# First attention laid out class by class: keys and queries stored by token mod 4, neighbour units reading keys in runs of 32, queries kept twice

## The chip, the cores and the metric

The kernel runs as one program on one core of a Trainium2 chip. The metric is the device time of one execution in microseconds (us), the median of several runs. Before the change it is 2000.86 us (3 runs, 2000.85 to 2000.86).

## What is computed

The reference is an encoder of two layers for 1024 tokens of width 1024. Each layer has a token-mixing part and a mixture of 16 experts; a final norm ends it. The change touches one part only: the dilated window attention of layer 0, with 12 heads of width 64. Cut to what matters:

```python
A_PATTERNS = ((128, 1), (512, 4), (2048, 16))

def dilated_band_attention(q, k, v, window, dilation):
    # query t attends t + j*dilation, |j| <= window/(2*dilation)
    ...
def dilated_mixture(q, k, v):
    results = [dilated_band_attention(q, k, v, w, d) for (w, d) in A_PATTERNS]
    outs = jnp.stack([o for (o, _) in results], axis=0)
    lses = jnp.stack([l for (_, l) in results], axis=0)
    wts = jax.nn.softmax(lses, axis=0)
    return jnp.einsum('pbsh,pbshc->bshc', wts.astype(q.dtype), outs)
```

Every head thus looks at its keys three times: 64 neighbours to each side; 64 to each side in steps of 4; 64 to each side in steps of 16. The weights of the mixture make it one softmax over all three sets of keys.

## The kernel before

**Units.** `a_attention` works through 12 heads, and each head through 8 units (96 in all, `u = 8*head + s`). A unit has two blocks of 128 queries by 256 keys. In units s = 0 to 3 (below: class units) r = s is a class of tokens, those with token mod 4 = r; a block takes 128 queries of the class against all its 256 keys, and one mask (`cls`) does the steps of 4 and of 16 together. In units s = 4 to 7 (neighbour units) a block takes 128 neighbouring queries against the 256 keys from 64 before to 64 behind them, under the masks `nat0` to `nat2`. The results of the class units go to `o2c`, those of the neighbour units to `o1`. `bounce` sends `o2c` through DRAM into the order of the tokens (`o2`), and four merge steps weigh the two.

**Precision.** Queries and keys are split into a high and a low part (`k.split`, L148 and L149), and the two halves of the 128 partitions hold hi and lo. `tr` transposes them on TensorE into a PSUM tile `apt` and copies that to `kT` and `qT`. `a_swap` writes a second copy of `kT` with hi and lo swapped, by two DMAs; a block's scores are two matmuls into one half of `ass` (L1190), one against each copy.

**Layout.** In `kT` the 1024 keys lie in the order of the tokens, with 64 zeros at either end; so do the queries in `qT`. A class unit reads both in steps of 4 elements (16 bytes, L1173 and L1174), a neighbour unit without a step (L1169).

**Order of the work.** The order is written by hand (`manual_schedule`): in step t the program emits the exponentials of unit t+1 (ScalarE, L1199), the four transposes of unit t (TensorE, `apP`, L1206) and the copy out of PSUM (ScalarE, `pT`, L1208), the scores of unit t+2 (TensorE) with the masking on VectorE (`sm`, L1192), the copies of the transposes asked for in the step before (`late`), the products with the values of unit t-1 (TensorE, `apO`, L1220) and, after each second one, a copy on VectorE (L1226). Then come the pieces of `prep` for a later head, by the table `plan`: splitting k and q, two transposes each for k and q (L1136, one `apt` of 4 matmuls), the swap. Each engine takes its instructions in this order.

**Loads.** SyncE's queue (SP) issues all loads of a head pair. `load` fetches `qs` and `ks` (one DMA each), `load_v` the values twice: `vc` by classes (four DMAs) and `vn` in runs of 128 tokens shifted by 64 (three DMAs, behind two small memsets on GpSimd). The swaps and the bounce are issued by the same queue, in program order: the swap of the next head stands behind the loads of the next pair. The first head is prepared earlier by `a_first`, while the projections of layer 0 still run.

Of the kernel before, what the change touches and what calls it, by code (L numbers as in the profile page):

```python
# [19 lines left out]
S = 1024  # L20
# [10 lines left out]
def _layout():  # L31
    parts = {}
    cols = []
    n = 0

    def add(name, a):
        nonlocal n
        a = np.asarray(a, np.float32).reshape(128, -1)
        parts[name] = (n, n + a.shape[1])
        cols.append(a)  # L40
        n += a.shape[1]

    p = np.arange(128)
    add("ident", np.eye(128))
    add("slots", np.broadcast_to(np.arange(1, 129), (128, 128)))
    add("pref", p[:, None] <= p[None, :])
    e16 = np.zeros((128, 16))
    e16[p[:32], p[:32] % 16] = 1.0
    add("e16", e16)
    add("prow", p)  # L50
    add("sgn", np.stack([np.where(p < 64, 1.0, -1.0), np.where(p < 32, 1.0, -1.0), np.where(p < 16, 1.0, -1.0)], 1))
    for m in (64, 32, 16):
        sel = np.zeros((128, m))
        sel[m:2 * m] = -np.eye(m)
        add(f"sel{m}", sel)
    w = np.arange(256)
    band = (w[None, :] >= p[:, None]) & (w[None, :] <= p[:, None] + 128)
    for name, ok in (("nat0", band & (w >= 64)), ("nat1", band), ("nat2", band & (w < 192))):
        add(name, np.where(ok, 0.0, NEG))
    cls = np.zeros((128, 2, 256))  # L60
    for hf in range(2):
        l = 128 * hf + p[:, None]
        cnt = (np.abs(l - w[None, :]) <= 64).astype(int) + ((l - w[None, :]) % 4 == 0)
        cls[:, hf] = np.where(cnt == 2, np.float32(np.log(2.0)), np.where(cnt == 1, 0.0, NEG))
    add("cls", cls)

    def table(pos, r, theta):
        half = r // 2
        inv = np.power(np.float32(theta), -np.arange(half, dtype=np.float32) * np.float32(2.0 / r))
        ang = pos.astype(np.float32)[:, None] * inv[None, :].astype(np.float32)  # L70
        return np.cos(ang).astype(np.float32), np.sin(ang).astype(np.float32)

    def chunked(t):
        return t.reshape(8, 128, -1).transpose(1, 0, 2)

    t = np.arange(S)
    for name, tabs in (("ra", [table(t, 16, 500000.0)]), ("rc", [table(t, 32, 500000.0)]),
                       ("rd", [table(t // 64, 32, 10000.0), table(t % 64, 32, 10000.0)])):
# [919 lines left out]
    return T  # L998


def a_keys(nc, qk, hp, qs, ks):
    src, c, w = (qk[0], hp * 128, 512) if hp < 4 else (qk[1], (hp - 4) * 128, 256)
    nc.sync.dma_start(qs, src[:, c:c + 128].rearrange("(c p) d -> p c d", p=128))
    nc.sync.dma_start(ks, src[:, w + c:w + c + 128].rearrange("(c p) d -> p c d", p=128))


def a_values(nc, vd, hp, vn, vc):
    nc.gpsimd.memset(vn[0:64, 0], 0.0)
    nc.gpsimd.memset(vn[64:128, 8], 0.0)
    vv = vd[:, 2 * hp:2 * hp + 2].rearrange("t h d -> t (h d)")  # L1010
    vr = vv.rearrange("(f p r) d -> p r f d", f=2, r=4)
    for r in range(4):
        nc.sync.dma_start(vc[:, 2 * r:2 * r + 2], vr[:, r])
    nc.sync.dma_start(vn[64:128, 0], vv[0:64])
    nc.sync.dma_start(vn[:, 1:8], vv[64:960].rearrange("(c p) d -> p c d", p=128))
    nc.sync.dma_start(vn[0:64, 8], vv[960:1024])
    return {n: t.rearrange("p c (h d) -> p c h d", h=2) for n, t in (("vn", vn), ("vc", vc))}


def a_swap(nc, kT):  # L1020
    for a in (0, 64):
        nc.sync.dma_start(*(kT[p:p + 64, f, 64:64 + S].bitcast(F32) for p, f in ((64 - a, 1), (a, 0))))


def a_first(k, qk, vd, pool, ps, cv):


    nc = k.nc

    def take(name, *shape, dtype=F32):  # L1030
        return pool.tile([128, *shape], dtype, name=name)
    kT, qT = take("kT", 2, 128 + S, dtype=F32R), take("qT", S, dtype=F32R)
# [4 lines left out]
    pair, head = dict(qs=qs, ks=ks, cls=cls), dict(kT=kT, qT=qT)  # L1037
# [8 lines left out]
    def trans(n, dst):  # L1046
        for half in range(2):
            pt = ps.tile([128, 4, 128], F32, name="pt").bitcast(F32R)
            for c in range(4):
                nc.tensor.transpose(pt[:, c], sp[n][:, 4 * half + c].rearrange("p a d -> p (a d)"), k.identr)  # L1050
            pv, sl = pt.rearrange("p a d -> p (a d)"), slice(half * 512, (half + 1) * 512)
            if half:
                nc.vector.tensor_copy(dst[:, sl], pv)
            else:
                nc.scalar.activation(dst[:, sl], pv, AF.Copy)

    def keys():
        trans(0, kT[:, 0, 64:64 + S])
        nc.vector.memset(kT[:, :, 0:64].bitcast(F32), 0.0)
        nc.vector.memset(kT[:, :, 64 + S:].bitcast(F32), 0.0)  # L1060
        split(1, qs)

    def queries():
        a_swap(nc, kT)
        trans(1, qT)
# [14 lines left out]
def a_attention(k, qk, vd, gd, o2d, start, late_work, ready):  # L1080
# [4 lines left out]
    with ExitStack() as ctx:  # L1085
# [26 lines left out]
        def prep(h):  # L1112
# [6 lines left out]
            def split_k():  # L1119
                sp = pq.tile([128, NCH, 2, 64], F32R, name="ksp", bufs=1)  # L1120
                k.split(sp[:, :, 0], sp[:, :, 1], pair[hp]["ks"][:, :, hs])
                d["ksp"] = sp
                d["kT"] = pk.tile([128, 2, 64 + S + 64], F32R, name="kT")
                nc.vector.memset(d["kT"][:, :, 0:64].bitcast(F32), 0.0)
                nc.vector.memset(d["kT"][:, :, 64 + S:].bitcast(F32), 0.0)
# [7 lines left out]
            def tr(dst, src, eng):  # L1133
# [3 lines left out]
                pv = pt.rearrange("p a d -> p (a d)")  # L1137
                if eng:
                    late.append(lambda: nc.vector.tensor_copy(dst, pv))
                else:  # L1140
                    late.append(lambda: nc.scalar.activation(dst, pv, AF.Copy))

            def tk(half):
                tr(d["kT"][:, 0, 64 + half * 512:64 + (half + 1) * 512], lambda c: d["ksp"][:, 4 * half + c], half)

            def tq(half):
                tr(d["qT"][:, half * 512:(half + 1) * 512], lambda c: d["qsp"][:, 4 * half + c], True)
# [10 lines left out]
        def blocks(u):  # L1158
# [1 line left out]
            h, s = divmod(u, 8)  # L1160
            hp, hh = divmod(h, 2)
            d, pr = head[h], pair[hp]
            qT, kT = d["qT"], d["kT"]
            out = []
            for j in range(2):
                if s >= 4:
                    c = 2 * (s - 4) + j
                    out.append((qT[:, c * 128:(c + 1) * 128], [kT[:, f, c * 128:c * 128 + 256] for f in range(2)],
                                k.c("nat0" if c == 0 else "nat2" if c == 7 else "nat1"),  # L1169
                                [pr["vn"][:, c + a, hh, 0:65] for a in range(2)], pr["o1"][:, c, hh]))  # L1170
                else:
                    r = s
                    out.append((qT.rearrange("p (l r) -> p r l", r=4)[:, r, j * 128:(j + 1) * 128],  # L1173
                                [kT[:, f, 64:64 + S].rearrange("p (l r) -> p r l", r=4)[:, r] for f in range(2)],  # L1174
                                pr["cls"][:, j], [pr["vc"][:, 2 * r + a, hh, 0:65] for a in range(2)],
                                pr["o2c"][:, 2 * r + j, hh]))
            return out
# [1 line left out]
        def emit_S(u):  # L1179
# [6 lines left out]
            ss = psS.tile([128, 2, 256], F32, name="ass")  # L1186
            sm = p3.tile([128, 2, 256], F32, name="sm")
            for j, (q, ks, mask, v, dst) in enumerate(bl):
                for f in range(2):
                    nc.tensor.matmul(ss[:, j], q, ks[f], start=(f == 0), stop=(f == 1))  # L1190
# [898 lines left out]
```

## Time and profile before

| | |
|---|---|
| median of 3 runs | 2000.86 us |
| the profiled execution's own time | 1999.71 us |
| its span, first to last instruction | 1997.9 us |
| TensorE matmul busy | 1864.8 us, 93% of the span |
| VectorE busy | 1473.5 us, 74% |
| ScalarE busy | 1244.9 us, 62% |
| mean granted TensorE clock | 0.968 |
| scores of the first attention (L1190), first and last start | 270.8 and 480.9 us |

The profile is of one execution. PE is TensorE's matmuls, PEld its weight loads, DVE is VectorE, ACT is ScalarE, POOL is GpSimd, SP is SyncE, whose rows are DMA issues. Times in rows count from the first instruction. The part that the change touches takes a little over a tenth of the span, from about 271 to 484 us; what precedes it (projections) and follows it (output projection, experts, layer 1) is the same program in both kernels.

### The profile page before, as it was taken

The page shows a single profiled execution, that of the slowest core. Times are in us where ns is not written, and L with a number is a line of the kernel's source. Part 1 is how long each engine was busy: PE and PEld are TensorE (multiplying, and loading weights), DVE is VectorE, ACT ScalarE, POOL GpSimd, SP SyncE. Part 2 cuts the span into 40 slices and gives each one's busy share as a digit, 9 for nine tenths or more (in the row PEclk, how much of TensorE's full clock was granted, in tenths as well). Part 3 has the DMA queues.
Part 4 walks back from the last instruction along what each step waited for, and adds up shares of the span by engine and source line. Part 5 has one row for each costly group of instructions (what it writes and reads, how often), then busy time and mean ns, then how long its engine had stood idle before and what let it go on. Part 6 is the DMA issues. An engine that isn't in the chain of part 4 may idle for free. (4 is left out here: it accounts for less than half of the span.)

```text
span 1997.9 us, 29943 instructions
## 1 busy us (share of the span) xinstructions
PE 1864.8 (93%) x10346; PEld 1568.7 (79%) x10346; DVE 1473.5 (74%) x3160; ACT 1244.9 (62%) x2022; POOL 352.4 (18%) x337
## 2 busy tenths in 40 slices
PE   8999999998995999998999799999997995999995
PEld 6888899997883788886888688888886873888884
DVE  6431246777557999997776688889996558999997
ACT  5322257776232888886634688889885334888884
POOL 0010010002002321211002233322212003212111
PEclk9999999999996999999899899999998997999997
DMA  7232354543473999995426554332213875999986
GB/s 236 69 106 75 116 153 130 140 108 109 158 261 126 377 389 384 385 395 156 134 70 202 114 75 90 60 50 42 53 22 93 288 256 201 391 387 385 387 332 229
DMA packets 214599, 386.32 MB, mean 193 GB/s; under 512 B 71984, under 2 KB 122928, under 8 KB 214448
## 3 DMA queue, kind: packets, MB, share of 16 engines
q1 hardware_dynamic: 190224, 303.95, 46.0%
q0 software_dynamic: 21488, 74.18, 12.2%
q10 hardware_dynamic: 2736, 6.29, 0.9%
q8 instruction: 81, 1.33, 0.3%
q14 instruction: 70, 0.57, 0.2%
HBM read 310.17 MB, written 66.85 MB: 189 GB/s over the span
## 5 line engine op out<-in xcount | busy, mean ns | idle before, releaser
L232 DVE TENSOR_TENSOR lo<-raw,hi 128x1024 fp32r<-128x1024 f32 x260 | 310.1, 1227 | 24.2 <-ACT hi L225 23.0
L225 ACT ACTIVATE hi<-raw 128x1024 fp32r<-128x1024 f32 x269 | 275.2, 1055 | 14.5 <-PE py L643 10.2
L259 PE MATMUL pp<-hi,hT 128*128 128x512 f32 (+2 forms) x576 | 213.4, 371 | 2.3 <-ACT hi L235 2.3
L260 PE MATMUL pp<-lo,hT 128*128 128x512 f32 (+2 forms) x576 | 211.8, 368 | 0.1
L261 PE MATMUL pp<-hi,hT 128*128 128x512 f32 (+2 forms) x576 | 211.4, 367 | 0.0
L1879 DVE TENSOR_REDUCE nm<-css 128x1 f32<-128x1024 f32 x128 | 156.0, 1218 | 41.5 <-PE css L1873 40.8
L149 DVE TENSOR_TENSOR PT<-cpt,PT 128x512 fp32r<-128x512 f32 x256 | 163.1, 678 | 6.1 <-ACT PT L148 3.8
L148 ACT ACTIVATE PT<-cpt 128x512 fp32r<-128x512 f32 x256 | 139.5, 597 | 42.1 <-PE cpt L1897 40.3
L1873 PE MATMUL css<-kT,qT 128*128 128x512 f32 x512 | 151.7, 398 | 10.7 <-ACT pe L1885 9.5
L1885 ACT ACTIVATE pe<-css,nm 128x1024 f32<-128x1024 f32 x128 | 143.6, 1122 | 11.0 <-DVE rinv L1905 7.1
L1897 PE MATMUL cpt<-csident,pe 128*128 128x128 f32 x1024 | 135.5, 275 | 1.0 <-DVE PT L149 0.9
L1897 PEld LDWEIGHTS cpt<-csident,pe 128*128 128x128 f32 x1024 | 117.1, 141 | 16.3 <-DVE PT L149 3.7
L1915 PE MATMUL po<-PT,vv 128*128 128x512 f32 x256 | 113.4, 443 | 13.2 <-DVE o L1923 13.2
L259 PEld LDWEIGHTS pp<-hi,hT 128*128 128x128 f32 x576 | 109.7, 190 | 19.8 <-ACT hi L235 2.7
L260 PEld LDWEIGHTS pp<-lo,hT 128*128 128x128 f32 x576 | 109.6, 190 | 17.8 <-DVE lo L236 0.8
L261 PEld LDWEIGHTS pp<-hi,hT 128*128 128x128 f32 x576 | 109.4, 190 | 17.5 <-DVE hT L149 0.2
L1873 PEld LDWEIGHTS css<-kT,qT 128*128 128x128 f32 x512 | 96.0, 189 | 34.6 <-ACT pe L1885 10.8
L1192 DVE CUSTOM_DVE_ANT_0 sm<-ass,csnat 128x256 f32<-128x256 f32 x176 | 67.3, 420 | 52.0 <-PE ass L1190 45.9
L578 POOL DMA_INDIRECT xs<-hd,idx x32 | 70.2, 2195 | 197.5 <-DVE gt L576 197.5
L1916 PE MATMUL po<-PT,vv 128*128 128x512 f32 x256 | 102.3, 400 | 0.0
L1190 PE MATMUL ass<-kT,qT 128*128 128x256 f32 x384 | 96.4, 381 | 1.0 <-DMA kT<-kT 1.0
L259 PE MATMUL pp<-hi,aTh 128*128 128x512 f32 x208 | 87.3, 420 | 0.4 <-DVE o L1226 0.4
(435 smaller groups left out, 4656.0 us busy)
## 6 DMA issues: line engine op xcount, KB each, us to landing
raw<-in_moe_w_up_dram SPq DMA_DIRECT2D x112, 512.0 KB
raw<-in_moe_w_down_dram SPq DMA_DIRECT2D x110, 512.0 KB
raw<-in_moe_w_gate_dram SPq DMA_DIRECT2D x106, 512.0 KB
attn<-in_moe_w_gate_dram SPq DMA_DIRECT2D x22, 512.0 KB
attn<-in_moe_w_down_dram SPq DMA_DIRECT2D x18, 512.0 KB
raw<-in_even_w_in_dram SPq DMA_DIRECT2D x16, 512.0 KB
hd<-h POOLq DMA_DIRECT2D x16, 512.0 KB, 6.0
attn<-in_moe_w_up_dram SPq DMA_DIRECT2D x16, 512.0 KB
```

Of the source, the lines that this page charges most:

```text
L148: self.nc.scalar.activation(hi, src, AF.Copy)
L149: (eng or self.nc.vector).tensor_tensor(lo, src, hi.bitcast(F32), op=ALU.subtract)
L225: nc.scalar.activation(hv, tv, AF.Copy)
L232: (nc.gpsimd if pool else nc.vector).tensor_tensor(lv, tv, hv.bitcast(F32), op=ALU.subtract)
L259: nc.tensor.matmul(out, ah, bh, start=first, stop=False)
L260: nc.tensor.matmul(out, ah, bl, start=False, stop=False)
L261: nc.tensor.matmul(out, al, bh, start=False, stop=last)
L1873: nc.tensor.matmul(ss[:, n], a[:, sl], m[:, n * 512:(n + 1) * 512], start=(j == 0), stop=(j == len(passes) - 1))
L1879: nc.vector.tensor_reduce(nm, B[b]["ss"], axis=AX.X, op=ALU.max, negate=True)
L1885: nc.scalar.activation(pe, B[b]["ss"], AF.Exp, bias=B[b]["nm"], accum_out=l)
L1897: nc.tensor.transpose(pt[:, kk], B[b]["pe"][:, kc * 128:(kc + 1) * 128], k.ident)
L1915: nc.tensor.matmul(po[g], vv[:, kc], PT[g][:, 0, kc], start=(kc == 0), stop=False)
```

## The change

- `a_keys` loads keys and queries class by class: a chunk of 128 rows now holds 128 tokens of one class. Each of the two loads becomes four DMAs, and the keys come first.
- `kT` becomes 4 classes of 256 keys with 16 zeros at either end of each. A class unit now reads queries and keys without a step.
- A neighbour unit reads its 256 keys as 2 x 4 runs of 32 elements (128 bytes): for each half of 128 tokens, 32 keys from each class. The masks' columns and the rows of `vn` are put in the same order; `vn` is loaded by 12 DMAs instead of 3, and its two memsets cover all 128 partitions.
- The neighbour units' queries have to be in the order of the tokens: a second tile `qN`, written from the same PSUM tile by another copy in steps of 4 elements: two ScalarE instructions for each of heads 1 to 11, two on VectorE for the first head.
- The swap moves four runs of 1 KB for each partition instead of one of 4 KB.

```diff
+    wk = 128 * (w // 128) + 4 * (w % 32) + w % 128 // 32
     for name, ok in (("nat0", band & (w >= 64)), ("nat1", band), ("nat2", band & (w < 192))):
-        add(name, np.where(ok, 0.0, NEG))
+        add(name, np.where(ok, 0.0, NEG)[:, wk])
...
+PAD = 16
 def a_keys(nc, qk, hp, qs, ks):
     src, c, w = (qk[0], hp * 128, 512) if hp < 4 else (qk[1], (hp - 4) * 128, 256)
-    nc.sync.dma_start(qs, src[:, c:c + 128].rearrange("(c p) d -> p c d", p=128))
-    nc.sync.dma_start(ks, src[:, w + c:w + c + 128].rearrange("(c p) d -> p c d", p=128))
+    for t, c0 in ((ks, w + c), (qs, c)):
+        v = src[:, c0:c0 + 128].rearrange("(f p r) d -> p r f d", f=2, r=4)
+        for r in range(4):
+            nc.sync.dma_start(t[:, 2 * r:2 * r + 2], v[:, r])
 def a_values(nc, vd, hp, vn, vc):
-    nc.gpsimd.memset(vn[0:64, 0], 0.0)
-    nc.gpsimd.memset(vn[64:128, 8], 0.0)
+    nc.gpsimd.memset(vn[:, 0], 0.0)
+    nc.gpsimd.memset(vn[:, 8], 0.0)
...
-    nc.sync.dma_start(vn[64:128, 0], vv[0:64])
-    nc.sync.dma_start(vn[:, 1:8], vv[64:960].rearrange("(c p) d -> p c d", p=128))
-    nc.sync.dma_start(vn[0:64, 8], vv[960:1024])
+    for r in range(4):
+        p = 32 * r
+        nc.sync.dma_start(vn[p + 16:p + 32, 0], vv[0:64].rearrange("(l r) d -> r l d", r=4)[r])
+        nc.sync.dma_start(vn[p:p + 32, 1:8], vv[64:960].rearrange("(c l r) d -> r l c d", l=32, r=4)[r])
+        nc.sync.dma_start(vn[p:p + 16, 8], vv[960:1024].rearrange("(l r) d -> r l d", r=4)[r])
 def a_swap(nc, kT):
     for a in (0, 64):
-        nc.sync.dma_start(*(kT[p:p + 64, f, 64:64 + S].bitcast(F32) for p, f in ((64 - a, 1), (a, 0))))
+        nc.sync.dma_start(*(kT[p:p + 64, f, :, PAD:PAD + 256].bitcast(F32) for p, f in ((64 - a, 1), (a, 0))))
+def a_pads(nc, kT):
+    nc.vector.memset(kT[:, :, :, 0:PAD].bitcast(F32), 0.0)
+    nc.vector.memset(kT[:, :, :, PAD + 256:].bitcast(F32), 0.0)
+def two(v):
+    return v.rearrange("p (r l) -> p r l", r=2)
...
             def tr(dst, src, eng, nat=None):
...
                 if eng:
                     late.append(lambda: nc.vector.tensor_copy(dst, pv))
                 else:
                     late.append(lambda: nc.scalar.activation(dst, pv, AF.Copy))
+                if nat is not None:
+                    late.append(lambda: nc.scalar.activation(nat, pv, AF.Copy))
...
                 if s >= 4:
-                    out.append((qT[:, c * 128:(c + 1) * 128], [kT[:, f, c * 128:c * 128 + 256] for f in range(2)],
+                    out.append((qN[:, c * 128:(c + 1) * 128],
+                                [kT[:, f, :, 32 * c:32 * c + 64].rearrange("p r (a l) -> p a r l", a=2) for f in range(2)],
...
-                    out.append((qT.rearrange("p (l r) -> p r l", r=4)[:, r, j * 128:(j + 1) * 128],
-                                [kT[:, f, 64:64 + S].rearrange("p (l r) -> p r l", r=4)[:, r] for f in range(2)],
+                    out.append((qT[:, 256 * r + j * 128:256 * r + (j + 1) * 128],
+                                [kT[:, f, r, PAD:PAD + 256] for f in range(2)],
```

On TensorE no instruction is added, dropped or moved. Two engines get more instructions.

ScalarE before, around the third head's split of k and q (`o_2336` is a buffer of `o1`, `pe` the exponentials, `pT` the copy of the transposed ones):

```order
104 L1199 ACTIVATE pe<-sm,o_2336 128x256 x2
105 L1208 ACTIVATE pT<-apP 128x512
106 L1199 ACTIVATE pe<-sm,o_2336 128x256 x2
107 L1208 ACTIVATE pT<-apP 128x512
108 L148 ACTIVATE ksp<-ks 128x8x64
109 L1199 ACTIVATE pe<-sm,o_2336 128x256 x2
110 L1208 ACTIVATE pT<-apP 128x512
111 L148 ACTIVATE qsp<-qs 128x8x64
```

and of the change, the same place:

```order
104 L1227 ACTIVATE pe<-sm,o_2354 128x256 x2
105 L1236 ACTIVATE pT<-apP 128x512
106 L1165 ACTIVATE qN<-apt 128x2x256
107 L1227 ACTIVATE pe<-sm,o_2354 128x256 x2
108 L1236 ACTIVATE pT<-apP 128x512
109 L1165 ACTIVATE qN<-apt 128x2x256
110 L150 ACTIVATE ksp<-ks 128x8x64
111 L1227 ACTIVATE pe<-sm,o_2354 128x256 x2
112 L1236 ACTIVATE pT<-apP 128x512
113 L150 ACTIVATE qsp<-qs 128x8x64
```

Two copies `qN<-apt` stand in front of the exponentials of the units that follow; everything else keeps its place.

SP's queue before, from the swap of one head over the loads of the next pair to the swap of the next head (`kT<-kT` is the swap, `o2d<-o2c` the bounce):

```order
36 L1022 DMA kT<-kT 64x1024 x2
37 L1003 DMA qs<-qka 128x8x128
38 L1004 DMA ks<-qka 128x8x128
39 L1013 DMA vc<-vd 128x2x132 x4
40 L1014 DMA vn<-vd 64x132
41 L1015 DMA vn<-vd 128x7x132
42 L1016 DMA vn<-vd 64x132
43 L1022 DMA kT<-kT 64x1024 x2
```

and of the change, from the same swap, as far as the fourth of twelve `vn` loads:

```order
54 L1033 DMA kT<-kT 64x4x256 x2
55 L1012 DMA ks<-qka 128x2x128 x4
56 L1012 DMA qs<-qka 128x2x128 x4
57 L1022 DMA vc<-vd 128x2x132 x4
58 L1025 DMA vn<-vd 16x132
59 L1026 DMA vn<-vd 32x7x132
60 L1027 DMA vn<-vd 16x132
61 L1025 DMA vn<-vd 16x132
```

Between the two swaps stand 24 load issues instead of 9, for the same bytes, the keys ahead of the queries.

## Rows read from the trace of the kernel before

**Rows 1.** The page, busy time of TensorE over the whole span (share, instructions)

```profile
PE 1864.8 (93%) x10346; PEld 1568.7 (79%) x10346; DVE 1473.5 (74%) x3160; ACT 1244.9 (62%) x2022; POOL 352.4 (18%) x337
```

**Rows 2.** Stretches (us): busy time of each engine (instructions), granted clock, DMA share, GB/s

```profile
410.00:445.00 35.00, 35.00 (x286) 34.95 (x285) 24.46 (x95) 24.90 (x55) 2.27 (x3) 1.00 0.49 123
445.00:480.00 35.00, 34.63 (x271) 33.83 (x270) 27.23 (x95) 26.94 (x56) 1.92 (x1) 1.00 0.22 62
```

**Rows 3.** Timeline of PE, scores only: start, us, line, tile, shape, count

```profile
307.63 1.29 PE L1190 MATMUL ass<-kT,qT 128*128 128x256 f32 x4
...
310.30 1.29 PE L1190 MATMUL ass<-kT,qT 128*128 128x256 f32 x4
...
312.63 1.29 PE L1190 MATMUL ass<-kT,qT 128*128 128x256 f32 x4
...
317.06 0.72 PE L1190 MATMUL ass<-kT,qT 128*128 128x256 f32 x4
...
319.15 0.72 PE L1190 MATMUL ass<-kT,qT 128*128 128x256 f32 x4
...
320.92 0.72 PE L1190 MATMUL ass<-kT,qT 128*128 128x256 f32 x4
...
340.53 1.29 PE L1190 MATMUL ass<-kT,qT 128*128 128x256 f32 x4
```

**Rows 4.** Groups by line, shape (262 to 490): count, busy us, mean ns

```profile
L1190 PE MATMUL ass<-kT,qT 128*128 128x256 f32 x384 | 96.4, 381 | 1.0 <-DMA kT<-kT 1.0
...
L1141 ACT ACTIVATE kT<-apt 128x512 fp32r<-128x512 f32 x11 | 6.4, 585 | 0.0
...
L261 PE MATMUL pp<-hi,hT 128*128 128x256 f32 x26 | 7.3, 281 | 0.0
...
L261 PE MATMUL pp<-hi,aTl 128*128 128x512 f32 x5 | 2.0, 395 | 0.0
```

**Rows 5.** Tile gpm (gMLP), operand in runs of 64: ns least/median/most

```profile
L261 PE MATMUL gpm<-vh,wT x4: 388/391/398, 114.7 to 133.6; 128*128 128x512 f32 x4
```

**Rows 6.** Timeline of SP's DMA issues, loads of the third pair

```profile
313.25 1.11 SPq L1022 DMA_DIRECT2D kT<-kT  x2
314.41 0.61 SPq L1003 DMA_DIRECT2D qs<-qka  x1
...
316.43 4.63 SPq L1013 DMA_DIRECT2D vc<-vd  x4
...
322.26 0.83 SPq L1016 DMA_DIRECT2D vn<-vd  x1
331.11 1.12 SPq L1022 DMA_DIRECT2D kT<-kT  x2
```

**Rows 7.** Timeline of ACT, same loads arriving [idle before, releaser]

```profile
319.14 0.91 ACT L1199 ACTIVATE pe<-sm,o 128x256 f32<-128x256 f32 x2 [0.19 <-DVE o L1192]
319.95 0.57 ACT L1208 ACTIVATE pT<-apP 128x512 f32<-128x512 f32 x1
...
323.31 0.63 ACT L148 ACTIVATE ksp<-ks 128x512 fp32r<-128x512 f32 x1 [1.43 <-DMA ks<-qka]
...
325.13 0.61 ACT L148 ACTIVATE qsp<-qs 128x512 fp32r<-128x512 f32 x1
```

**Rows 8.** Timeline of PE, second head's first scores

```profile
285.89 0.57 PE L1190 MATMUL ass<-kT,qT 128*128 128x256 f32 x1
287.46 1.05 PE L1190 MATMUL ass<-kT,qT 128*128 128x256 f32 x3 [0.99 <-DMA kT<-kT]
```

**Rows 9.** Timeline of SP, that head's swap

```profile
282.24 1.12 SPq L1022 DMA_DIRECT2D kT<-kT  x2
```

**Rows 10.** Line L399, ACT reading in steps of 2 elements

```profile
L399 ACT ACTIVATE h<-xt,rstd x2: 1194/1195/1196, 614.8 to 1646.6; 128x1024 f32<-128x1024 f32 x2
```

**Rows 11.** The page, a dense ACT copy of that size

```profile
L225 ACT ACTIVATE hi<-raw 128x1024 fp32r<-128x1024 f32 x269 | 275.2, 1055 | 14.5 <-PE py L643 10.2
```

**Rows 12.** Timeline of DVE, near the end of the stage

```profile
462.03 1.94 DVE L232 TENSOR_TENSOR lo<-raw,hi 128x1024 fp32r<-128x1024 f32 x1
```

More of the change, by code (lines that the diff above doesn't have):

```diff
@@ L1031, in take @@
         return pool.tile([128, *shape], dtype, name=name)
-    kT, qT = take("kT", 2, 128 + S, dtype=F32R), take("qT", S, dtype=F32R)
+    kT, qT, qN = take("kT", 2, 4, 2 * PAD + 256, dtype=F32R), take("qT", S, dtype=F32R), take("qN", S, dtype=F32R)
     qs, ks = take("qs", NCH, 128), take("ks", NCH, 128)
@@ L1036, in a_first @@
     sp = {}
-    pair, head = dict(qs=qs, ks=ks, cls=cls), dict(kT=kT, qT=qT)
+    pair, head = dict(qs=qs, ks=ks, cls=cls), dict(kT=kT, qT=qT, qN=qN)
     def load():
@@ L1050, in trans @@
                 nc.tensor.transpose(pt[:, c], sp[n][:, 4 * half + c].rearrange("p a d -> p (a d)"), k.identr)
-            pv, sl = pt.rearrange("p a d -> p (a d)"), slice(half * 512, (half + 1) * 512)
+            pv, rs = two(pt.rearrange("p a d -> p (a d)")), slice(2 * half, 2 * half + 2)
             if half:
-                nc.vector.tensor_copy(dst[:, sl], pv)
+                nc.vector.tensor_copy(dst[:, rs], pv)
             else:
-                nc.scalar.activation(dst[:, sl], pv, AF.Copy)
+                nc.scalar.activation(dst[:, rs], pv, AF.Copy)
+            if nat is not None:
+                nc.vector.tensor_copy(nat[:, rs], pv)
     def keys():
-        trans(0, kT[:, 0, 64:64 + S])
-        nc.vector.memset(kT[:, :, 0:64].bitcast(F32), 0.0)
-        nc.vector.memset(kT[:, :, 64 + S:].bitcast(F32), 0.0)
+        trans(0, kT[:, 0, :, PAD:PAD + 256])
+        a_pads(nc, kT)
         split(1, qs)
@@ L1064, in queries @@
         a_swap(nc, kT)
-        trans(1, qT)
+        trans(1, qT.rearrange("p (r l) -> p r l", r=4), qN.rearrange("p (l r) -> p r l", r=4))
     def rest():
@@ L1122, in split_k @@
                 d["ksp"] = sp
-                d["kT"] = pk.tile([128, 2, 64 + S + 64], F32R, name="kT")
-                nc.vector.memset(d["kT"][:, :, 0:64].bitcast(F32), 0.0)
-                nc.vector.memset(d["kT"][:, :, 64 + S:].bitcast(F32), 0.0)
+                d["kT"] = pk.tile([128, 2, 4, 2 * PAD + 256], F32R, name="kT")
+                a_pads(nc, d["kT"])
             def split_q():
@@ L1131, in split_q, with tr @@
                 d["qT"] = pk.tile([128, S], F32R, name="qT")
-            def tr(dst, src, eng):
+                d["qN"] = pk.tile([128, S], F32R, name="qN")
+            def tr(dst, src, eng, nat=None):
                 pt = psT.tile([128, 4, 128], F32R, name="apt")
@@ L1136, in tr @@
                     nc.tensor.transpose(pt[:, c4], src(c4).rearrange("p a d -> p (a d)"), k.identr)
-                pv = pt.rearrange("p a d -> p (a d)")
+                pv = two(pt.rearrange("p a d -> p (a d)"))
                 if eng:
@@ L1141, in tr @@
                     late.append(lambda: nc.scalar.activation(dst, pv, AF.Copy))
+                if nat is not None:
+                    late.append(lambda: nc.scalar.activation(nat, pv, AF.Copy))
             def tk(half):
-                tr(d["kT"][:, 0, 64 + half * 512:64 + (half + 1) * 512], lambda c: d["ksp"][:, 4 * half + c], half)
+                tr(d["kT"][:, 0, 2 * half:2 * half + 2, PAD:PAD + 256], lambda c: d["ksp"][:, 4 * half + c], half)
             def tq(half):
-                tr(d["qT"][:, half * 512:(half + 1) * 512], lambda c: d["qsp"][:, 4 * half + c], True)
+                rs = slice(2 * half, 2 * half + 2)
+                tr(d["qT"].rearrange("p (r l) -> p r l", r=4)[:, rs], lambda c: d["qsp"][:, 4 * half + c], True,
+                   d["qN"].rearrange("p (l r) -> p r l", r=4)[:, rs])
             L[0].append(split_k)
@@ L1162, in blocks @@
             d, pr = head[h], pair[hp]
-            qT, kT = d["qT"], d["kT"]
+            qT, qN, kT = d["qT"], d["qN"], d["kT"]
             out = []
@@ L1188, in emit_S @@
             for j, (q, ks, mask, v, dst) in enumerate(bl):
+                o = ss[:, j] if len(ks[0].shape) == 2 else ss[:, j].rearrange("p (a r l) -> p a r l", a=2, r=4)
                 for f in range(2):
-                    nc.tensor.matmul(ss[:, j], q, ks[f], start=(f == 0), stop=(f == 1))
+                    nc.tensor.matmul(o, q, ks[f], start=(f == 0), stop=(f == 1))
             for j, (q, ks, mask, v, dst) in enumerate(bl):
```

2 lines of the change are left out of this document (1 added, 1 removed).

## Prediction

> **What bounds the kernel now.** I read the page first: matmuls are busy for 93% of the span [rows 1], so a stage is paid for by TensorE unless its own rows say otherwise. The stage of the change lies between 270.8 us (first scores) and about 484 us. The busy times by stretch are the second view [rows 2]: between 410 and 445 us PE is busy for 35.00 of 35 us at a granted clock of 1.00 (the 2.4 GHz level), VectorE for 24.46, ScalarE for 24.90, the DMA engines for about half. The three stretches of 35 us before it read alike; the last one, 445 to 480, is different: VectorE 27.23, PE 34.63.
>
> The third view is PE's timeline, scores alone [rows 3]. From the first matmul of one unit's scores to that of the next, I read 2.67 us (307.63 to 310.30) and 2.33 (310.30 to 312.63) behind class units, 2.09 (317.06 to 319.15) and 1.77 (319.15 to 320.92) behind neighbour units; the longer of each pair has four extra transposes of `prep` in it. These four periods recur almost to the hundredth all along the stage. PE therefore never waits there; it sets the pace. A class unit costs 2.33 - 1.77 = 0.56 or 2.67 - 2.09 = 0.58 us more, although it does the same number of columns: its four score matmuls take 1.29 us against 0.72. What differs is the step of 16 bytes in both operands.
>
> **The change, part by part.**
>
> *Class units without a step.* 12 heads x 4 units = 48. If each comes down to a neighbour unit's period, PE saves 48 x 0.57 = 27.4 us. The bounds: all of it, or nothing, if something else than the step made them slow. I take all: dense matmuls of 256 columns with two-part operands take 281 ns on this PE, the mean of the scores is 381 [rows 4], which is what half slow and half dense gives.
>
> *Neighbour units in runs of 32.* No row shows runs of 32. The gMLP's matmuls read 512 columns in runs of 64 and take 391 ns [rows 5]; dense ones of that size take 395 [rows 4]. So runs of 64 cost nothing. The other end is that runs of 32 cost as much as a step of 4 does, 0.57 us for each of 48 neighbour units. I take nothing, since 32 is far nearer to 64 than to 1.
>
> The SBUF page of the Trainium skill ("SBUF — State Buffer", Door 1: The DMA port swizzle) says that memory lines are 16 bytes wide, that an access in the same line goes at full speed and a crossing to a new line is penalised. It also says that one may step over 4 fp32 values for free; by that the class units would not be slow and the change would be worth 0. Rows 3 show 1.29 us against 0.72 at just this step, so I hold to the first half of the rule. By that half, runs of 32 fill 8 whole lines, but each value of `qN` goes to a line of its own, which is the first rival's case.
>
> *The copies to `qN`.* 22 on ScalarE. A dense copy of that size out of PSUM takes 585 ns [rows 4]. ScalarE rows with a step know only 8 bytes: 1195 ns for 1024 elements [rows 10] against 1055 dense [rows 11], 13% more. Bounds: 0.585 (no price) and 1.17 us (doubled, as the class scores nearly are); I take 0.6. The cover is ScalarE's idle time. A pair of heads is 16 units; 8 x 1.77 + 8 x 2.33 + 8 x 0.33 = 35.4 us now, 30.9 after. ScalarE does about 24.90 x 35.4/35 = 25.2 us per pair, and 27.6 with four copies: 89% of the new period. VectorE comes to 24.7 us, 80%. So the sums fit, but locally it is narrow: five units in a row of each head have an extra ScalarE instruction (two qN, two splits, one key copy). A unit's copy starts 0.81 us after its exponentials and takes 0.57 [rows 7], 1.38 together; with 0.585 for the extra one five units are 9.83 us, and PE needs 2.1 + 1.77 + 1.77 + 2.1 + 2.1 = 9.84. Just hidden, and the three units that follow have nothing extra. If that cover is gone, what ScalarE has over is PE's wait. The two VectorE copies for the first head fall into a time in which VectorE waits for the first scores: nothing.
>
> *Loads on SP.* Now the 9 load issues of a pair run from 314.41 to 323.09, the next swap is issued at 331.11, 17.86 us after the last one [rows 6]. Four class units lie between the swaps, so the next swap will be due 15.6 us after the last. After it about 9.7 us pass before its scores want it (first scores of that head at 340.53 [rows 3], second matmul a little later), since only neighbour units lie there. The swap's own landing is read at the second head: issue at 282.24 [rows 9], the second score matmul runs only at 287.46 behind DMA `kT<-kT` [rows 8], 5.2 us. So the loads may end about 4.5 us after the swap is due: 15.6 + 4.5 - 1.2 = 18.9 us for 24 issues, 0.79 each. An unhindered issue takes 0.61; where the queue is backed up, the four of `vc` take 4.63, 1.16 each [rows 6]. Bounds of the 24: 8.7 us (same bytes) and 27.8. I take 24 x 0.6 = 14.4: no wait. The one new wait among them, `vn` on GpSimd's memset, has `vn` loads, the next swap and the bounce behind it, but the memset runs while SP still issues `vc`.
>
> *Keys first.* Now `ks`, behind `qs`, lands when its split begins, at 323.31 after 1.43 us of idle ScalarE [rows 7]. Afterwards the keys' 512 KB go first and the queries land at about 323.3; their split is called at 325.13 now, at about 325.13 - 1.43 = 323.7 once ScalarE need not wait for the keys. Hidden with little to spare. The 1.43 us themselves buy nothing, since PE did not wait.
>
> *Where class units gain less.* At the start, loads that wait for the buffers stand ahead of the second head's swap, while the four first class units bring its use about 2 us nearer; today PE waits 0.99 us for it [rows 8]. Bounds 0 to 2 us lost; I take 1. At the end, VectorE is nearly full (27.23 us [rows 2]), with splits of weights of 1.94 us [rows 12] between the masks; 8 class units are emitted in that stretch, 4.6 us. I count 2 as lost, bounds 0 to 4.
>
> Sum: 27.4 - 1 - 2 = 24.4, and 0.4 for small waits of the five later pairs: 24.0. The profiled execution takes 1999.71 us (its span 1997.9 and 1.8 around it), so 1975.7; it stands 1.15 us under the median of the runs, so 1976.9 for the median. I say 1977. Nothing behind the stage changes and its loads hang on instructions of the stage, so it moves forward as it is.
>
> **Rivals.**
>
> *ScalarE takes over.* If writing in steps doubles the copies, the five units need 9.83 + 2 x 0.585 = 11.0 us against PE's 9.84: 1.16 late per head, 13 us over 11 heads. Scores are emitted two units ahead and absorb some of it; I take half, 6.5: 1983.5, and 1990 at the worst. For: 16 bytes is the step at which PE slows. Against: PE at that step still takes 256 columns in 1.29/4 = 0.32 us, 0.8 per ns, and the copy asks for 512 elements in 0.585 us, 0.9 per ns.
>
> *The change does not do what it says.* If runs of 32 are as slow as steps, 48 x 0.57 come back: 2001, no change. Against: rows 5.
>
> *SP's queue becomes the bound.* Place: swap of the next head behind 24 issues. At 1.16 us each they end 27.8 us after they begin, 8.9 later than allowed; five pairs make 45 us, less the 24 gained: 2022. It costs from 0.79 us per issue on and outweighs the gain from about 0.99 (18.9 + 24/5 = 23.7 us for 24). For: rows 6 hold issues of that length. Against: those were held up by bytes ahead of them, which are the same bytes in both kernels.
>
> **How the numbers follow.** The forecast gets 0.70, ScalarE 0.14, no change 0.06, SP 0.10. The forecast's own range is 1972.5 (no loss: 2000.86 - 27.4 = 1973.5, and the 0.99 us of rows 8) to 1981 (start and end at their worst). To hold 8 in 10 it has to reach over the middle of ScalarE's case: 1972.5 to 1987. A difference under 0.2% (4 us) cannot be told from none here. Faster 0.85, same 0.05, slower 0.10.
>
> **What would show it.** Class units' scores in 0.72 us and their periods 1.77 and 2.1; neighbour units unchanged at 0.72 (if they rise to 1.29, the second rival). `qN` copies near 0.6 us and no idle PE behind `pe`; if PE waits for exponentials in the units after them, the first rival. The SP row from a pair's first load to the next swap shorter than 17 us, and no score matmul behind `kT<-kT` except at the second head; if there are such waits in each pair, the third. The forecast is wrong if the stage, 210 us from first to last scores, shrinks by less than 18.

## The result and the profile after

The changed kernel takes 1985.81 us (median of 4 runs, 1981.82 to 1987.59) against 2000.86 before: ratio 0.9919, 95% interval 0.9902 to 0.9936. Its profiled execution took 1985.63 us (span 1983.6). On another chip, run again (the fifth experiment), it took 1981.89 against 1991.50: 0.9953, 0.9936 to 0.9969. The time lies inside the range 1972.5 to 1987, 9 us above the 1977 forecast; but in the part that was changed, it will be seen, only a third of the forecast gain arrived (7.8 of 24 us).

The page's busy times, which answer to [rows 1]: ScalarE's have gone up by 13.6 us, TensorE's down by 19.1.

```profile
PE 1845.7 (93%) x10346; PEld 1541.2 (78%) x10346; DVE 1471.7 (74%) x3162; ACT 1258.5 (63%) x2044; POOL 351.7 (18%) x337
```

Busy times by stretch (columns as in [rows 2]):

```profile
410.00:445.00 35.00, 33.84 (x294) 31.65 (x292) 26.60 (x98) 29.27 (x60) 2.20 (x3) 1.00 0.53 139
445.00:480.00 35.00, 31.35 (x246) 29.84 (x246) 21.49 (x79) 26.35 (x52) 3.30 (x2) 0.90 0.13 33
```

TensorE is no longer busy all the time: 33.84 of 35 us where it had 35.00. ScalarE went from 24.90 to 29.27. In the last stretch the granted clock is 0.90: a spell at 0.5 (1.2 GHz) begins at 456 us and lasts 6.8, at a place where the kernel before had none.

The groups by line between 262 and 490 us, which answer to [rows 4]:

```profile
L1218 PE MATMUL ass<-kT,qT 128*128 128x256 f32 x192 | 35.0, 305 | 0.8 <-DMA kT<-kT 0.8
L1218 PE MATMUL ass<-kT,qN 128*128 128x256 f32 x192 | 34.7, 302 | 0.0
L1165 ACT ACTIVATE qN<-apt 128x512 fp32r<-128x512 f32 x22 | 24.1, 1096 | 14.7 <-DVE qT L1161 14.7
```

Class units (`qT`) and neighbour units (`qN`) now cost TensorE the same, 69.7 us together against 96.4. But a copy into `qN` takes 1096 ns, not 600, and in front of these copies ScalarE sat idle for 14.7 us, until VectorE's copy `qT` was done. (The records of neighbouring instructions overlap a little, so the busy time of ScalarE grows by less than the 24.1 us of the copies.)

How the size and the wait reach TensorE is seen in the second pair of heads, while the queries of its second head are prepared, in three timelines (start, us, ..., idle before and its releaser). ScalarE:

```profile
313.99 0.58 ACT L1236 ACTIVATE pT<-apP 128x512 f32<-128x512 f32 x1
315.65 1.10 ACT L1165 ACTIVATE qN<-apt 128x512 fp32r<-128x512 f32 x1 [1.08 <-DVE qT L1161]
316.54 0.87 ACT L1227 ACTIVATE pe<-sm,o 128x256 f32<-128x256 f32 x2
```

VectorE, the copy that it waited for:

```profile
314.94 0.68 DVE L1161 CAST qT<-apt 128x512 fp32r<-128x512 f32 x1
```

TensorE:

```profile
314.77 0.71 PE L1218 MATMUL ass<-kT,qN 128*128 128x256 f32 x4
315.32 1.00 PE L1248 MATMUL apO<-vc,pT 128*128 128x65 f32 x8
317.07 0.83 PE L1234 MATMUL apP<-csident,pe 128*128 128x128 f32 x4 [0.74 <-ACT pe L1227]
317.65 0.73 PE L1218 MATMUL ass<-kT,qN 128*128 128x256 f32 x4
...
319.80 0.72 PE L1218 MATMUL ass<-kT,qT 128*128 128x256 f32 x4
...
322.08 0.71 PE L1218 MATMUL ass<-kT,qT 128*128 128x256 f32 x4
...
324.17 0.72 PE L1218 MATMUL ass<-kT,qT 128*128 128x256 f32 x4
```

ScalarE is free at 314.57, the queries' transposes have ended, but the copy begins at 315.65, right behind VectorE's (314.94 to 315.62). It takes 1.10 us; the exponentials behind it begin at 316.54, and the transposes that need them idle 0.74 us. The period 314.77 to 317.65 is 2.88 us, where [rows 3] have 1.77 for a neighbour unit without `prep`.

The waits of the whole stage (engine, line, waited for: us in total, times, longest):

```profile
PEld apP L1234 <- ACT pe L1227: 15.0, 41, 2.3
ACT qN L1165 <- DVE qT L1161: 14.7, 12, 1.5
...
PE apP L1234 <- ACT pe L1227: 7.6, 10, 2.1
```

The time from the first unit's scores to the last unit's is called the stage below. Its two ends before, and then after the change:

```profile
270.80 2.15 PE L1190 MATMUL ass<-kT,qT 128*128 128x256 f32 x8
...
480.51 0.72 PE L1190 MATMUL ass<-kT,qT 128*128 128x256 f32 x4
```

```profile
271.23 1.11 PE L1218 MATMUL ass<-kT,qT 128*128 128x256 f32 x8
...
473.18 0.72 PE L1218 MATMUL ass<-kT,qN 128*128 128x256 f32 x4
```

The stage went from 209.7 to 201.95 us, 7.8 us less, and the second pair of heads (from unit 16's scores to unit 32's, "the pair" below) from 35.58 to 33.49. The other 7 us of the first comparison lie behind the stage, in unchanged code (see the section on why the prediction was right and wrong).

### The profile page after: what moved, and what is told of

Read it like the earlier page. It is cut to its first block, busy times and chain, and to the rows that moved or that the text cites. A ratio compares the mean times of both kernels' runs of the same rounds, so it can differ in the third digit from the quotient of the medians.

```text
span 1983.6 us, 30146 instructions
## 1 busy us (share of the span) xinstructions
PE 1845.7 (93%) x10346; PEld 1541.2 (78%) x10346; DVE 1471.7 (74%) x3162; ACT 1258.5 (63%) x2044; POOL 351.7 (18%) x337
## 5 line engine op out<-in xcount | busy, mean ns | idle before, releaser
L227 ACT ACTIVATE hi<-raw 128x1024 fp32r<-128x1024 f32 x269 | 275.3, 1055 | 14.3 <-PE py L645 9.5
L150 ACT ACTIVATE xh<-tp 128x512 fp32r<-128x512 f32 x64 | 38.1, 599 | 78.3 <-PE tp L590 52.4
```

Of the source, the lines that this page charges most:

```text
L150: self.nc.scalar.activation(hi, src, AF.Copy)
L227: nc.scalar.activation(hv, tv, AF.Copy)
```

## The experiments

Theory 1: ScalarE's queue, with the size of the copies into `qN` and the wait ahead of each, paces the units and eats most of the gain. Rivals: the gain is lost at the stage's end and in the clock; or to SP's queue. Runs with a ratio are each compared with the kernel before on the same chip; its median was 1994.51 us for e1 to e4, 1991.50 for e5 to e8, 2004.61 for e9 to e12. e8, e10, e11 and e12 ran once each, so their totals have no interval; their stages are compared, which in the two profiles of the changed kernel differ by 0.15 us.

**e1, no copy into `qN`.**

```diff
-                if nat is not None:
-                    late.append(lambda: nc.scalar.activation(nat, pv, AF.Copy))
...
-                    out.append((qN[:, c * 128:(c + 1) * 128],
+                    out.append((qT[:, c * 128:(c + 1) * 128],
```

> The changed kernel without any copy into qN: the neighbour units read qT, so their queries are the wrong ones (this part of the computation is changed). Theory 1 (the 22 ScalarE copies of 1.1 us, each with about 0.67 us of waiting for VectorE's qT copy ahead of it, pace the units): the pair of heads from unit 16 to unit 32 goes from 33.49 us to 30.8 to 31.5, the wait of the probabilities' transposes for ScalarE's pe falls from 15 us to under 4, and the attention's stage is 12 to 18 us shorter than in the changed kernel, total 1968 to 1975. Rival (the gain is lost at the end of the stage and in the clock, not to the copies): the pair stays at 33 or more, total 1981 to 1987. Rival (the 24 loads of the queue): loads are all still there, so nothing changes, 1981 to 1987.

1967.82 us, ratio 0.9873 (0.9853 to 0.9892). The stage's end:

```profile
457.86 0.72 PE L1214 MATMUL ass<-kT,qT 128*128 128x256 f32 x4
```

From 270.83 us on, where its first scores start, the stage takes 187.0 us, 14.9 less than in the changed kernel; the second and third pair take 31.02 and 31.24. TensorE's weight loads still wait a little more than the 4 us expected:

```profile
PEld apP L1230 <- ACT pe L1223: 5.2, 14, 0.8
```

Theory 1 holds; the loads are all still there, so the rival with the queue falls. Near the stage's end, the five periods from unit 84's scores to unit 89's, 16.57 us in the changed kernel and 11.29 before, take 12.70, and there is no clock spell among them: most of what was lost there came with the copies too.

**e2, the copies written densely.**

```diff
...
-                   d["qN"].rearrange("p (l r) -> p r l", r=4)[:, rs])
+                   d["qN"].rearrange("p (r l) -> p r l", r=4)[:, rs])
```

> The copies stay, but qN is written densely, in class order, so the neighbour units' queries are the wrong ones (this part of the computation is changed). Theory 1a (the size: a write with a step of 16 bytes takes 1.1 us and a dense one 0.59): 22 x 0.51 = 11 us of ScalarE go, the pair falls from 33.49 to 31 to 32, total 1973 to 1979. Theory 1b (the wait: each copy still stands in ScalarE's queue for 0.67 us until VectorE's copy of the same tile is done): the pair stays within 0.7 us of 33.49, total 1981 to 1986. Rival (neither): unchanged, and the copies' own duration stays at 1.1 us if the price is not the write's step but reading in two blocks.

1973.18 us, ratio 0.9900 (0.9880 to 0.9919); stage 194.2, pair 32.37. The copies take 596 ns and still wait:

```profile
L1165 ACT ACTIVATE qN<-apt 128x512 fp32r<-128x512 f32 x22 | 13.1, 596 | 15.9 <-DVE qT L1161 15.9
```

Taking the size away alone gives back 7.7 us of the stage, about half of what the copies cost.

**e12, the wait moved.** The natural counterpart to e2: the size stays, ScalarE's copy goes first.

```diff
+                if nat is not None:
+                    late.append(lambda: nc.scalar.activation(nat, pv, AF.Copy))
                 if eng:
                     late.append(lambda: nc.vector.tensor_copy(dst, pv))
                 else:
                     late.append(lambda: nc.scalar.activation(dst, pv, AF.Copy))
-                if nat is not None:
-                    late.append(lambda: nc.scalar.activation(nat, pv, AF.Copy))
```

> As the changed kernel, but ScalarE makes its copy (step of 16 bytes, 1.1 us) first and VectorE's copy of the same tile waits for it: the wait of 0.67 us per copy leaves ScalarE, the size stays, and VectorE stands 1.1 us in its place, with the masks behind it. Theory 1 with ScalarE as the only pace-setter: 22 x 0.67 = 15 us of its idle time go, the first to last unit falls from 201.9 to 194 to 198 us. Rival (either engine's queue paces the units, and the wait is only moved): 200 to 205 us.

One run: 1982.58 us, stage 194.5. ScalarE's copy starts as soon as the one before it ends (the place shown above):

```profile
312.58 0.57 ACT L1236 ACTIVATE pT<-apP 128x512 f32<-128x512 f32 x1
313.06 1.10 ACT L1161 ACTIVATE qN<-apt 128x512 fp32r<-128x512 f32 x1
313.94 0.86 ACT L1227 ACTIVATE pe<-sm,o 128x256 f32<-128x256 f32 x2
```

The wait is not gone but moved. VectorE now waits before its own copy, and in each of four pairs TensorE's transposes of the keys wait for VectorE's split of k, which stands behind that copy:

```profile
DVE qT L1163 <- ACT qN L1161: 10.9, 22, 0.8
...
PE apt L1158 <- DVE ksp L151: 4.3, 4, 1.1
```

That costs less: with the wait off ScalarE the stage is 7.5 us shorter, about as much as the size gave. The two do not simply add up, as e7 and e9 will show.

**e3, queries in natural order alone, read in steps by the class units.** There is no `qN` and no copy into it.

```diff
-    for t, c0 in ((ks, w + c), (qs, c)):
...
+    nc.sync.dma_start(qs, src[:, c:c + 128].rearrange("(c p) d -> p c d", p=128))
...
-                    out.append((qT[:, 256 * r + j * 128:256 * r + (j + 1) * 128],
+                    out.append((qT.rearrange("p (l r) -> p r l", r=4)[:, r, j * 128:(j + 1) * 128],
```

> Keys and values as in the changed kernel, queries as in the kernel before: one natural load, qT in natural order, no qN; class units load their queries into TensorE with a step of 16 bytes. Theory 1 with a free step on the weights' side: class units' four score products stay at 0.72 us, the pair is 30.8 to 31.5, total 1967 to 1975. Rival (the step costs the loaded operand what it cost the moving one): class units take 0.95 to 1.29 us again, up to 48 x 0.57 = 27 us come back of which the copies' 15 are saved, total 1980 to 1999.

1985.91 us, ratio 0.9962 (0.9947 to 0.9977); stage 205.0. The rival holds: the four products of a class unit take 1.19 us.

**e8, the other way round: the kernel before, its queries read densely, keys in steps.**

```diff
-                    out.append((qT.rearrange("p (l r) -> p r l", r=4)[:, r, j * 128:(j + 1) * 128],
+                    out.append((qT[:, 256 * r + j * 128:256 * r + (j + 1) * 128],
```

> The kernel before, with the class units' queries read densely (their queries are then the wrong ones; this part of the computation is changed), keys still in steps of 16 bytes. The strided queries alone gave 1.19 us for a class unit's four products, both in steps 1.29, neither 0.72. If the two prices lie beside each other (weights load while the last product streams): 1.2 to 1.29 us, total within 3 us of before. Rival (they add up): 0.72 + 0.10 = 0.82 us, some 20 us faster.

One run: 1988.77 us, stage 204.8, four products 1.17 us. Three class units of e3 between 305 and 313 us, then the same of e8 (PE the products, PEld the weight loads; mean ns):

```profile
L1214 PE MATMUL ass<-kT,qT 128*128 128x256 f32 x13 | 4.0, 417 | 0.0
L1214 PEld LDWEIGHTS ass<-kT,qT 128*128 128x128 f32 x12 | 3.0, 325 | 0.0
```

```profile
L1190 PE MATMUL ass<-kT,qT 128*128 128x256 f32 x12 | 3.5, 441 | 0.0
L1190 PEld LDWEIGHTS ass<-kT,qT 128*128 128x128 f32 x12 | 2.2, 200 | 0.1
```

Either step alone gives nearly the full price (1.19 and 1.17 of 1.29, against 0.72): stepped queries lengthen the weight load to 325 ns (dense 190), stepped keys the product, and the two lie beside each other. Taking one away gives 4.7 to 4.9 us of the stage; the rest of the 27.4 us comes only with both, so for that the change does need a second copy of the queries, or something in its place.

**e4, the copies on GpSimd, from `qT` in SBUF.**

```diff
-                    late.append(lambda: nc.scalar.activation(nat, pv, AF.Copy))
+                    late.append(lambda: nc.gpsimd.tensor_copy(nat, dst))
```

> Everything as in the changed kernel, but the 22 copies into qN of the later heads are made by GpSimd, from qT in SBUF. Theory 1: ScalarE is free of 24 us of copies and 15 us of waiting, nobody stands behind GpSimd's copy, and the neighbour units need it some 8 us later: pair 30.8 to 31.7, total 1968 to 1976. Rival (the copies' cost is not ScalarE's queue): as the changed kernel, 1981 to 1987. Rival (GpSimd's copy takes over 4 us and the first neighbour unit waits for it, or it slows VectorE's masks): the products ass show a wait for qN, and the total is 1980 or more.

1974.86 us, ratio 0.9905 (0.9889 to 0.9922); stage 196.0, pair 32.42, 34.98 in a pair with a clock spell. No score waits for `qN`. Some of the gain goes elsewhere: GpSimd's merge step follows its copy, and a VectorE product that runs beside it takes twice the 1214 ns that it takes in e1. VectorE's split of k stands behind that product, and TensorE waits for it:

```profile
L1296 DVE TENSOR_TENSOR attn<-o,ww 128x1024 f32<-128x1024 f32 x2 | 5.1, 2538 | 0.0
```

```profile
PE apt L1158 <- DVE ksp L151: 5.5, 4, 1.4
```

**e5, the changed kernel again.** No edit.

> The changed kernel itself, beside the kernel before on the same chip. Theory 1: its units take the same times again (pair 33.5 us, first to last unit 201.9, matching products at the stage's end some 6 us earlier than before). If the further 8 us that the first comparison showed behind the attention come from the change, the ratio is again 0.990 to 0.994 and they are there again; if they belonged to that one profile of the kernel before, the runs of before on this chip lie nearer, and the ratio is 0.994 to 0.998.

Stage 201.8, pair 33.52: as before, to a few hundredths. But the ratio does not settle the rest: 0.9953 lies in the second of the two ranges, its interval (0.9936 to 0.9969) reaches into the first.

**e6, the copies on VectorE.**

```diff
-                    late.append(lambda: nc.scalar.activation(nat, pv, AF.Copy))
+                    late.append(lambda: nc.vector.tensor_copy(nat, pv))
```

> As the changed kernel, but the second copy of the queries is made by VectorE, right behind its own first copy: no engine waits for another, ScalarE has 24 us less, VectorE has 22 x 1.08 = 24 us more. Theory 1 (ScalarE's queue paces the units): pair 31.3 to 32.5, first to last unit 189 to 196, total 1970 to 1977. Rival (VectorE has no room: 27.7 of 35 us without the copies, 4.3 more for each pair, and masks stand behind the copies): the pair is 33 or more, total 1981 or more.

Theory 1 missed, and the rival holds: 1982.32 us, ratio 0.9959 (0.9948 to 0.9971), stage 202.0, pairs 33.15 to 34.60. VectorE pays 1096 ns per copy, is busy for 30 of 35 us, and TensorE waits elsewhere (clock spells of 3.4 us in two of the pairs add to it):

```profile
375.00:410.00 35.00, 33.19 (x309) 32.87 (x307) 30.10 (x108) 26.94 (x61) 2.21 (x3) 1.00 0.51 131
```

```profile
PE apt L1158 <- DVE ksp L151: 7.2, 4, 1.8
```

So it is not ScalarE as such: on either of the two engines the 24 us of copies make TensorE wait.

**e7, queries in runs of 32 as well, both copies on VectorE.** The neighbour units' queries are kept class by class within each block, so that the second copy writes runs of 128 bytes.

```diff
+        add(name, np.where(ok, 0.0, NEG)[4 * (p % 32) + p // 32][:, wk])
...
+                    late.append(lambda: nc.vector.tensor_copy(nat, pv.rearrange("p r (c l) -> p r c l", l=32)))
...
+            for r in range(4):
+                nc.sync.dma_start(d["o2"][32 * r:32 * r + 32].rearrange("p c h d -> p c (h d)"),
+                                    o2d[hp].rearrange("(c l r) h d -> r l c (h d)", l=32, r=4)[r])
...
-            k.nc.tensor.transpose(pt[:, kk], self.attn[:, c, (4 * q + kk) * 128:(4 * q + kk + 1) * 128], k.ident)
+            k.nc.tensor.transpose(pt[:, kk], self.attn[:, c, (4 * q + kk) * 128:(4 * q + kk + 1) * 128], k.identp)
...
```

> The neighbour units' queries also in runs of 32 by class (their masks' rows in the same order), so that the second copy is written in runs of 128 bytes: on VectorE, 0.69 us each. o1 then has its rows in that order; o2 and the gate's columns are loaded in it (four loads for one), and the permuted identity of attn's transposes puts the tokens back. Theory 1: 22 x 0.69 = 15 us of VectorE, no wait between engines: pair 31.0 to 31.9, first to last unit 187 to 192, total 1967 to 1973. Rival (the added loads or the transposes take it back): the merge or attn waits for o2 or the gate's columns, 1975 or more.

1972.62 us, ratio 0.9905 (0.9889 to 0.9922); stage 193.4, pair 32.10, both a little over what was expected. The copies take 680 ns each, and what is left over e1's pair is once more TensorE's wait for VectorE's split of k, 1.07 of 1.09 us in the second pair:

```profile
L1165 DVE CAST qN<-apt 128x512 fp32r<-128x512 f32 x22 | 15.0, 680 | 0.0
```

```profile
PE apt L1158 <- DVE ksp L151: 4.4, 4, 1.1
```

**e9, the same with one engine for both copies of a tile.** ScalarE makes both of the first half, VectorE both of the second. The diff is against e7.

```diff
-                    late.append(lambda: nc.vector.tensor_copy(nat, pv.rearrange("p r (c l) -> p r c l", l=32)))
+                    rl = pv.rearrange("p r (c l) -> p r c l", l=32)
+                    late.append((lambda: nc.vector.tensor_copy(nat, rl)) if eng else (lambda: nc.scalar.activation(nat, rl, AF.Copy)))
...
-                tr(d["qT"].rearrange("p (r l) -> p r l", r=4)[:, rs], lambda c: d["qsp"][:, 4 * half + c], True,
+                tr(d["qT"].rearrange("p (r l) -> p r l", r=4)[:, rs], lambda c: d["qsp"][:, 4 * half + c], half,
```

> As the run with the queries in runs and both copies on VectorE, but each transposed tile has one engine for both of its copies: ScalarE the first half, VectorE the second. No wait between the two; ScalarE gets 2 x 0.6 us per pair and half more, VectorE nothing above the kernel before. Theory 1c (what was left with dense copies, 7 us over the kernel without copies, was mostly the wait): first to last unit 188 to 191 us, pair 31.0 to 31.9, total 1967 to 1971. Rival (it was the copies themselves, wherever they are): 192 to 195 us as with both on VectorE (193.4) or dense with the wait (194.2), total 1971 to 1976.

1980.10 us beside 2004.61: ratio 0.9883 (0.9867 to 0.9898), the largest gain of a kernel that computes all of the reference, though its interval overlaps those of e4 and e7. Its stage takes 192.9 us; theory 1c expected 188 to 191, so the rival, 192 to 195, holds. Without the wait and without the step, the copies still cost 5.9 us over e1. About 1.2 of these belong to one pair (33.46 against 32.0), where a swap came late behind the loads; of the two waits in this row the longest, 1.4, is that of the second head, which the other kernels have too:

```profile
PE ass L1223 <- DMA kT<-kT: 2.6, 2, 1.4
```

**e11, another order in the write.**

```diff
-                    late.append(lambda: nc.scalar.activation(nat, pv, AF.Copy))
+                    late.append(lambda: nc.scalar.activation(nat, pv.rearrange("p r l -> p l r"), AF.Copy))
...
-                   d["qN"].rearrange("p (l r) -> p r l", r=4)[:, rs])
+                   d["qN"].rearrange("p (l r) -> p l r", r=4)[:, :, rs])
```

> As the changed kernel, with the second copy made in another order: for each l both classes of the tile, so that two neighbouring floats (8 bytes) of each 16 are written one after the other, read from the tile 256 floats apart. If what costs is each jump between lines of 16 bytes in the write, a copy falls from 1.1 us to 0.6 to 0.85 and the first to last unit from 201.9 to 195 to 199 us. If every float written or read off the dense order costs its own time, it stays at 1.1 or grows.

One run: 1990.06 us, stage 194.7. The copy drops to 636 ns, though it reads its operand in jumps of 1 KB:

```profile
L1165 ACT ACTIVATE qN<-apt 128x512 fp32r<-128x512 f32 x22 | 14.0, 636 | 15.8 <-DVE qT L1161 15.8
```

With every write 16 bytes behind the one before it took 1096 ns, with two neighbours in a row 636, dense 596: the same 512 elements. A cost for each element off the dense order does not fit that. Nor does one fixed cost for each jump: e11 has half as many jumps, which at one price each would leave 250 of the extra 500 ns, and 40 are left. Two neighbouring writes at a place take nearly the whole price away; why is not shown.

**e10, the kernel before again.** No edit.

> The kernel before on this chip, with a profile. If the further 8 us behind the attention belonged to the first profile of before and not to the change, its attention takes 209.7 us again, and the rest behind it is 4 to 9 us shorter than in that profile; total 1988 to 1998. If they belong to the change: the rest is as long as there, and the total is 2000.

One run: 2012.20 us; neither expectation holds. Its stage is the same but for a clock spell of 10.2 us in the first pair (213.2; the four pairs behind it take 35.4 to 35.6). What lies behind the stage is even longer than in the first profile: 1525.8 us from the last unit's scores against 1517.4.

## Why the prediction was right and wrong

**Right: what bounded the kernel, and what a step costs.** Class units came down to 0.72 us and runs of 32 cost nothing. Without copies (e1) the stage shrinks by 22.7 us, against 27.4 - 1 - 2 = 24.4 for the sum without its last term, and the second pair by 35.58 - 31.02 = 4.56, which is 8 x 0.57 exactly. The start lost 0.85 us of the 1 allowed (30.44 for the first pair, 34.15 before), the last pair 2.3 where 2 were allowed (31.30 against 33.55), and the pairs between them 1.5 where 0.4 had been put.

**Right: SP's queue.** In the changed kernel the 24 loads and the swap behind them, which answer to [rows 6]:

```profile
310.77 2.92 SPq L1012 DMA_DIRECT2D ks<-qka  x4
...
329.22 1.26 SPq L1033 DMA_DIRECT2D kT<-kT  x2
```

18.45 us from the first load to the swap, 0.77 for each of the 24 where 0.6 had been taken. That is just under the 18.9 that were said to be the limit (the 17 named as a sign was too strict), and no score waits behind a swap except at the second head (0.76 us, 0.99 in [rows 8]). The limit is real, though: in e9 these loads took 20.7 us at the same place, and TensorE waited 1.2 us for the swap.

**Wrong: the copies to `qN`.** They were taken at 0.6 us, hidden, with 0.4 us for all small waits. They cost 201.95 - 187.03 = 14.9 us of the stage, as e1 shows. Two things failed. The size: a copy takes 1.10 us, near the upper bound of 1.17; "against" in the first rival compared rates of two engines, which said nothing about the write. And a term that was not in the sum at all: the wait. The copy reads the same PSUM tile as VectorE's `qT` copy, and the program lets the second reader wait for the first; on ScalarE it stood ahead of the exponentials. The prediction asked for such a wait on SP's queue, not here. By its own mark (a stage that shrinks by less than 18) the forecast was wrong, and its first rival is what happened, at over twice the 6.5 us given to it, since it had the doubled size alone. (The 1981 given for start and end at their worst is 1980 by its own terms; nothing hangs on it.)

**How the two halves add up.** Stage times: 201.95 with both; 194.2 without the size (e2); 194.5 without the wait on ScalarE (e12); 192.9 and 193.4 without either (e9, e7); 187.0 without the copies (e1). Either relief gives 7 to 8 us, both together only 9. The second pair, which has no clock spell in any of these runs, says the same: 33.49 with both, 32.36 and 32.42 with one relief, 32.10 and 32.01 with both, 31.02 without copies. Of the 7.7 and 7.5 us, 2.6 and 3.7 come in the last pair alone, where e2 and e12 do not have the changed kernel's clock spell. What stays behind ScalarE's overload is VectorE's: in e12, e4 and e7 TensorE's longest new wait is for the split of k on VectorE, 4.3 to 5.5 us of the stage, which e1 does not have. e9 and e7 also move queries, loads and merges, so that last split is less clean than the first.

**In range partly by luck.** The prediction said that what lies behind the stage moves forward as it is. It did not: of the 14.3 us between the two profiled spans, 7.8 are in the stage; some 7 lie behind it, in code that is the same. With the stage's 7.8 us alone the time would have been about 1993 us, outside the range. From the last unit's scores to the end of the span: 1517.4 us before, 1510.4 after. One place can be named: in the second layer's attention, TensorE's wait for a VectorE result, before and after:

```profile
PE po L1915 <- DVE o L1923: 8.9, 1, 8.9
```

```profile
PE po L1943 <- DVE o L1951: 1.5, 1, 1.5
```

In the first profile it stands behind a load, `aT<-oda`, for which ScalarE waited 8.2 us. In e10 that wait is 10.0 us and in e8, the other kernel with the old loads, 6.0; in the ten other profiles with the new layout 1.5 to 2.6. The new layout thus goes with a shorter wait 1000 us later. Of its 7.4 us only 3.5 are left 20 us behind it, by the starts of the same matmuls in the two profiles; another 3.4 had come before it, from about 1084 us on. But the whole rest varies more than that: 1505 to 1512 us on the chips of e1 to e8, 1514 to 1526 on that of e9 to e12. In the second comparison 9.6 us in total face 7.9 in the stage (209.7 against e5's 201.8). What sets this later part was not isolated and stays open; so does the reason for the clock spell at 456 us, which e5 shows at the same place (455.9).

## What to carry to other kernels

When a change gives a tile a second reader on another engine, look at what that copy waits for and what stands behind it in its queue: here the wait cost as much as the doubled size, and swapping two lines (e12) moved it to an engine on which it cost less. Price a copy by the pattern of its writes, not by its element count alone (the same 512 elements took 596, 636 and 1096 ns), and where a small engine sum "just fits", check it unit by unit with waits included. A gain in total time counts as the change's own only where the stage's own timeline shows it.

## What the runs showed of the hardware

- A write in steps of 16 bytes costs VectorE as much as ScalarE: 1096 ns for 128x512 (e6) against 680 in runs of 128 bytes (e7); on ScalarE 1096 against 596 dense (e2). GpSimd's copy with the same step, read from SBUF and not from PSUM, took 1152 ns in the median (e4, 1120 to 2124).
- A weight load in steps of 16 bytes takes 325 ns against 190; beside stepped products of 441 ns it adds little, as far as e3, e8 and the kernel before show: removing one of the two steps gave 0.10 to 0.12 us of 0.57.
- A transpose on TensorE takes a permutation in place of the identity and reorders on the way: in e7 and e9 it puts the tokens back, with 10346 matmuls as before.
